# A batched float32 matmul on one Trainium2 core: the last row tile of the first x sent as transfers of four, five and six partitions and one of 48

## The chip, the cores and the metric

The kernel runs on one core of a Trainium2 chip. The metric is the device time of one execution in microseconds (us), lower is better; a time is the median of several executions, and their range is given. "Span" is the profiled execution from its first to its last instruction; it is about 1.8 us shorter than the time that is measured from outside. All multi-run results here were classed as the fast state by the run records. A profile shows one execution only, and a single run is of unknown state.

Ratios are computed as the mean time of one kernel's runs over the mean time of the other's runs of the same rounds.

## The reference

```python
def setup_inputs():
    batch, m, k, n = 32, 512, 1024, 768
    return {"x": np.random.randn(batch, m, k).astype(np.float32),
            "weight": np.random.randn(batch, k, n).astype(np.float32)}

def reference(x, weight):
    return np.matmul(x, weight).astype(np.float32)
```

There are 32 independent products of a 512x1024 with a 1024x768 matrix. Everything has to come from memory once and go back once: the profile counts 167.77 MB read and 50.33 MB written.

## The kernel before

Loads of x and of the weights go out on the GpSimd queue, which converts float32 to bfloat16 on the way, and stores of all but the last four batches go out there too. One load is different. The first x is brought in as float32 on SyncE's queue, in three parts: its first three row tiles (128 partitions x 3 rows), then 96 rows of the last row tile in sixteen transfers of six, then its last 32 rows in one. A "row" in this text is one partition's share of that last row tile: 1024 float32, 4096 bytes.

```python
    def load_x(b):
        xs[b] = x_pool.tile([P, MT, K], BF16, name="x_sb")
        nc.gpsimd.dma_start(out=xs[b], in_=x_view[b])
    # ... load_w(b): the weights of batch b, the same way
    # ... transpose, matmuls, evacuate: TensorE transposes, bf16 matmuls, copies out of PSUM

    with tc.manual_schedule():
        x_first = first_pool.tile([P, MT, K], F32)

        nc.sync.dma_start(x_first[:, :MT - 1], x_view[0, :, :MT - 1])
        for block in range(0, 96, 24):
            for at in range(block, block + 4):
                few = slice(at, block + 24, 4)          # six partitions, four apart
                nc.sync.dma_start(x_first[few, MT - 1], x_view[0, few, MT - 1])
        nc.sync.dma_start(x_first[96:, MT - 1], x_view[0, 96:, MT - 1])
        load_w(0)
        # ... identity; loads of x 1, w 1, x 2, w 2, x 3
        for b in range(B):
            # ... loads ahead and stores behind, on the GpSimd queue
            if b == B - 1:          # six stores of the last four batches go on SyncE's queue
                nc.sync.dma_start(out_view[b - 1, :, halves[0]], outs[b - 1][:, halves[0]])
                for late in range(B - LATE, B - 2):
                    nc.sync.dma_start(out_view[late], outs[late])
                nc.sync.dma_start(out_view[b - 1, :, halves[1]], outs[b - 1][:, halves[1]])
            # ... transposes and matmuls of batch b; after each pair of the last batch:
            #     nc.sync.dma_start(out_view[b, :, halves[pair]], outs[b][:, halves[pair]])
```

SyncE's queue thus carries 1 + 17 + 6 = 24 transfers. The framework gives them eight completion semaphores in turn, so the ninth transfer waits for the first one's semaphore, and so on. The first transposes wait for all sixteen strided transfers, although they read other row tiles.

Of the kernel before, what the change touches and what calls it, by code (L numbers as in the profile page):

```python
# [12 lines left out]
@with_exitstack  # L13
def kernel(
    ctx: ExitStack,
    tc: tile.TileContext,
    x: bass.AP,
    weight: bass.AP,
    out: bass.AP,
):  # L20
    nc = tc.nc
    B, M, K = x.shape
    _, _, N = weight.shape
    P = 128
    MT = M // P
    KT = K // P
    JT = KT // 2
    N2 = 2 * N
    CHUNKED = {B - 4: (4, 4), B - 3: (4, 4), B - 2: (4, 4), B - 1: (4, 2, 2)}
    AHEAD = 3  # L30
    LATE = 4
    HELD = 3

    const = ctx.enter_context(tc.tile_pool(name="const", bufs=1))
    first_pool = ctx.enter_context(tc.tile_pool(name="first", bufs=1))
    w_pool = ctx.enter_context(tc.tile_pool(name="w", bufs=4))
    x_pool = ctx.enter_context(tc.tile_pool(name="x", bufs=5))
    xT_pool = ctx.enter_context(tc.tile_pool(name="xT", bufs=8))
    out_pool = ctx.enter_context(tc.tile_pool(name="out", bufs=7))
    tpsum = ctx.enter_context(tc.tile_pool(name="tpsum", bufs=2, space=bass.MemoryType.PSUM))  # L40
    mpsum = ctx.enter_context(tc.tile_pool(name="mpsum", bufs=2, space=bass.MemoryType.PSUM))



    w_view = weight.rearrange("b (ki ko) n -> b ki ko n", ki=P)
    x_view = x.rearrange("b (mi mo) k -> b mi mo k", mi=P)
    out_view = out.rearrange("b (mi mo) n -> b mi (mo n)", mi=P)

    xs, ws, outs = {}, {}, {}

    def banks():
        return [mpsum.tile([P, 512], F32, name=f"pm{i}") for i in range(3)]
# [5 lines that stand above are left out]
    def load_w(b):  # L58
        ws[b] = w_pool.tile([P, KT, N], BF16, name="w_sb")
        at = 0  # L60
        for n in CHUNKED.get(b, (KT,)):
            nc.gpsimd.dma_start(out=ws[b][:, at:at + n, :], in_=w_view[b, :, at:at + n, :])  # L62
            at += n

    def transpose(b, mt):

        pt = tpsum.tile([P, JT, P], F32, name="pt")
        pairs = xs[b].bitcast(F32)
        for j in range(JT):
            nc.tensor.transpose(pt[:, j, :], pairs[:, mt, j::JT], ident)  # L70
        xT = xT_pool.tile([P, JT, P, 2], BF16, name="xT")
        nc.vector.tensor_copy(  # L72
            xT.rearrange("p j m r -> p (j m r)"), pt.bitcast(BF16).rearrange("p j m -> p (j m)")
        )
        return xT

    def transpose_first(mt):

        xT = xT_pool.tile([P, JT, P, 2], BF16, name="xT")
        for h in range(2):  # L80
            pt = tpsum.tile([P, JT, P], F32, name="pt")
            for i in range(JT):
                nc.tensor.transpose(pt[:, i, :], x_first[:, mt, JT * h + i::KT], ident)  # L83
            nc.vector.tensor_copy(  # L84
                xT[:, 2 * h:2 * h + 2].rearrange("p j m r -> p j r m"),
                pt.rearrange("p (j r) m -> p j r m", r=2),
            )
        return xT



    SPLITS = (
        ((0, 0, 0, 512), (1, 0, 512, N - 512)),
        ((1, N - 512, 0, 1024 - N), (2, 0, 1024 - N, N2 - 1024)),
    )

    def matmuls(pm, half, xT, b, kos, together):
        for ko in kos:
            for i, (bank, at, off, size) in enumerate(SPLITS[half]):
                shares = half == 1 and i == 0  # L100
                nc.tensor.matmul(  # L101
                    pm[bank][:, at:at + size],
                    xT[:, ko // 2, :, ko % 2],
                    ws[b][:, ko, off:off + size],
                    start=(ko == 0 and not (together and shares)),
                    stop=(ko == KT - 1),
                    skip_group_check=together,
                )

    def evacuate(b, pair, pm):  # L110
        o = outs[b][:, pair * N2:(pair + 1) * N2]
        nc.scalar.copy(o[:, 0:512], pm[0])  # L112
        nc.vector.tensor_copy(o[:, 512:1024], pm[1])  # L113
        nc.scalar.copy(o[:, 1024:N2], pm[2])  # L114

    with tc.manual_schedule():
        x_first = first_pool.tile([P, MT, K], F32)

        nc.sync.dma_start(x_first[:, :MT - 1], x_view[0, :, :MT - 1])
        for block in range(0, 96, 24):  # L120
            for at in range(block, block + 4):
                few = slice(at, block + 24, 4)
                nc.sync.dma_start(x_first[few, MT - 1], x_view[0, few, MT - 1])
        nc.sync.dma_start(x_first[96:, MT - 1], x_view[0, 96:, MT - 1])
        load_w(0)
        ident = const.tile([P, P], F32)
        make_identity(nc, ident)
        for b in range(1, AHEAD):
            load_x(b)
            load_w(b)  # L130
        load_x(AHEAD)

        pending = []
        for b in range(B):
            if b + AHEAD + 1 < B:
                load_x(b + AHEAD + 1)
            if b + AHEAD < B:
                load_w(b + AHEAD)
            if b <= B - LATE:
                if b > 0:  # L140
                    pending.append(b - 1)
                if b + AHEAD < B - HELD or b == B - LATE:
                    for at in pending:
                        nc.gpsimd.dma_start(out=out_view[at], in_=outs[at])  # L144
                    pending = []
            if b == B - 1:
                halves = [slice(pair * N2, (pair + 1) * N2) for pair in range(2)]
# [4 lines that stand above are left out]
            outs[b] = out_pool.tile([P, MT * N], F32, name="out_sb")  # L152
            if b not in CHUNKED:
                turn = transpose if b else lambda _, mt: transpose_first(mt)
                xT = {mt: turn(b, mt) for mt in (0, 1)}
                for pair in range(2):
                    pm = banks()
                    for half in range(2):
                        if pair == 0:
                            matmuls(pm, half, xT[half], b, range(KT), False)  # L160
                            xT[2 + half] = turn(b, 2 + half)
                        else:
                            matmuls(pm, half, xT[2 + half], b, range(KT), False)
                    evacuate(b, pair, pm)
                continue
            xT = {0: transpose(b, 0)}
            pms = [banks() for _ in range(2)]
            at = 0
            for n in CHUNKED[b]:
                last = at + n == KT  # L170
                for mt in range(MT):
                    if mt + 1 not in xT and mt + 1 < MT:
                        xT[mt + 1] = transpose(b, mt + 1)
                    matmuls(pms[mt // 2], mt % 2, xT[mt], b, range(at, at + n), True)
                    if last and mt % 2 == 1:
                        pair = mt // 2
                        evacuate(b, pair, pms[pair])
                        if b == B - 1:
                            nc.sync.dma_start(out_view[b, :, halves[pair]], outs[b][:, halves[pair]])
                at += n  # L180
# [30 lines left out]
```

## Time and profile before

| | before |
|---|---|
| median of 6 runs (range) | 517.36 us (516.30 to 517.49) |
| span of the profiled run | 515.7 us |
| memory traffic | 423 GB/s over the span |
| DMA engines, share of busy time | 90% or more in 38 of 40 slices |
| first transpose | 33.6 us |
| first and last increment of the last store | 508.21 and 514.34 us |

The page of the kernel before, parts 1 to 3. The digits are 40 equal slices of the span in tenths of busy time; part 3 has packets, MB and share of 16 engines for each queue.

```profile
span 515.7 us, 5952 instructions
...
PE   0039999999999988779879779887898976999990
...
DMA  8999999999999999999999999999999999999996
...
q0 software_dynamic: 13824, 126.88, 96.7%
q1 hardware_dynamic: 1248, 8.39, 4.1%
q8 instruction: 20, 0.33, 0.2%
...
HBM read 167.77 MB, written 50.33 MB: 423 GB/s over the span
```

The DMA line is what bounds the kernel: nine tenths and more from the second slice to the last but one. TensorE (PE) starts only in the third slice and has gaps. Note the small line of q8: 20 packets of instructions, 0.2% of the engines' time.

The view of waits of the kernel before (engine, line, what it waited for: us in total, times, longest):

```profile
PE pm L101 <- DMA w_sb<-in_weight_dram: 43.9, 17, 4.4
...
PE pt L83 <- DMA x_first<-in_x_dram: 33.6, 1, 33.6
```

TensorE waits for weights that are late, and at the start for the small pieces of the first x.

SyncE's timeline of the kernel before (start us, us, what):

```profile
0.74 0.39 SPq L119 DMA_DIRECT2D x_first<-in_x_dram  x1
1.19 20.33 SPq L123 DMA_DIRECT2D x_first<-in_x_dram  x16
22.62 0.36 SPq L124 DMA_DIRECT2D x_first<-in_x_dram  x1
```

The share of busy time does not say which of the 16 engines ends last. The semaphore increments do, since each transfer gets one increment from every engine that it uses. The trace records them with their times, but not with the engine's number. Below are increments of three transfers on the GpSimd queue and of the last store, as the first increment's time and the others' delay behind it, sorted:

```
before
load at  14.10  0.08 0.22 0.33 0.40 0.42 0.43 0.50 0.50 0.54 0.77 0.83 0.85 0.87 0.89 0.99
load at  43.59  0.06 0.23 0.31 0.37 0.39 0.41 0.47 0.48 0.51 2.74 2.78 2.82 2.84 2.86 2.97
load at  55.73  0.07 0.24 0.32 0.37 0.45 0.46 0.47 0.48 0.51 2.74 2.80 2.81 2.85 2.95 3.93
last st 508.21  0.29 0.53 2.71 2.79 2.81 2.92 2.94 3.15 3.19 3.39 3.54 3.71 3.97 4.81 6.13
```

At 43.59 us six engines are about 2.5 us behind the other ten: those that carried the small transfers. By 55.73 us one of the six is a further 1.1 us late (2.86 to 3.93); one 16 KB instruction packet had passed at 49.7 us. In this trace none of it is made up: at 123.80 us four of the late engines still stand at 2.73 to 2.85 us, and the first increments come in the same rhythm to the end (3.65 to 3.68 us for each store, for example). Each load and store of the GpSimd queue increments once from each of the 16 engines, so a delay stays to the end. In the last store one engine is 6.13 us behind. Its tail can be seen in the profile too, in the view by windows (window, length, busy us of the compute engines, TensorE clock, DMA share, GB/s):

```profile
508.00:510.00 2.00, 0.00 (x0) 0.00 (x0) 0.00 (x0) 0.00 (x0) 0.00 (x0) 0.50 0.84 350
510.00:512.00 2.00, 0.00 (x0) 0.00 (x0) 0.00 (x0) 0.00 (x0) 0.00 (x0) 0.50 0.45 187
512.00:514.00 2.00, 0.00 (x0) 0.00 (x0) 0.00 (x0) 0.00 (x0) 0.00 (x0) 0.50 0.07 31
```

From 508 us on nothing computes. From 512 to 514 us a share of 0.07 of 16 engines is about one engine.

### The profile page before, as it was taken

Reading aid. Unit: us, or ns where it says so; the run is one execution under the profiler, and the core shown is the slowest. Engines: PE = TensorE matmul, PEld = TensorE weight load, DVE = VectorE, ACT = ScalarE, POOL = GpSimd, SP = SyncE. Lnnn points to the kernel's source line nnn. Section 1 sums busy time; section 2 is a strip of 40 time slices with the busy share of each in tenths; the row PEclk is TensorE's granted clock in tenths of the full one; section 3 lists DMA queues with packets and bytes.
Section 4 is the critical chain, followed back from the end, with each engine's and each line's share of the span. In section 5 each row is a group of like instructions: output and inputs, shape, how many; then the busy total and the mean of one; then the engine's idle time right before and its main releaser. Section 6 shows DMA issues by size and latency. Waiting matters only on the chain.

```text
span 515.7 us, 5952 instructions
## 1 busy us (share of the span) xinstructions
PE 417.8 (81%) x2528; PEld 276.1 (54%) x2576; DVE 129.9 (25%) x196; ACT 76.2 (15%) x129; POOL 51.7 (10%) x102
## 2 busy tenths in 40 slices
PE   0039999999999988779879779887898976999990
PEld 0036666666666655446546455554564644566660
DVE  0023333333333313122223231322331322133330
ACT  0001111111111111111101111110110111111110
POOL 3000111111001010100101001100111010111000
PEclk9999999999999989899979998898997998899996
DMA  8999999999999999999999999999999999999996
GB/s 234 223 225 216 218 272 275 260 243 270 277 274 268 243 261 278 275 273 248 250 275 276 275 259 244 271 274 276 272 240 260 277 275 272 250 244 214 300 426 257
DMA packets 15097, 135.64 MB, mean 263 GB/s; under 512 B 1760, under 2 KB 1760, under 8 KB 3552
## 3 DMA queue, kind: packets, MB, share of 16 engines
q0 software_dynamic: 13824, 126.88, 96.7%
q1 hardware_dynamic: 1248, 8.39, 4.1%
q8 instruction: 20, 0.33, 0.2%
q14 instruction: 5, 0.04, 0.0%
HBM read 167.77 MB, written 50.33 MB: 423 GB/s over the span
## 4 chain that ended last, share of the span: by engine, by line
DMA 63%; PE 30%; DVE 3%; issue 1%; ACT 0%; POOLq 0%
PE pm L101 27%; DMA w_sb<-in_weight_dram 25%; DMA out_dram<-out_sb 16%; DMA x_sb<-in_x_dram 16%; DMA x_first<-in_x_dram 6%; PE pt L70 2%; DVE out_sb L113 1%; DVE xT L72 1%; PE pt L83 1%; ACT out_sb L114 0%; POOLq L144 0%; POOLq L62 0%; POOLq L56 0%
## 5 line engine op out<-in xcount | busy, mean ns | idle before, releaser
L101 PE MATMUL pm<-w_sb,xT 128*128 128x256 bf16 (+1 forms) x2000 | 363.4, 336 | 51.3 <-DMA w_sb<-in_weight_dram 43.9
L101 PEld LDWEIGHTS <-xT 128*128 128x128 bf16 x2048 | 204.5, 101 | 185.8 <-issue 52.9
L72 DVE COPY xT<-pt 128x1024 bf16<-128x1024 bf16 x124 | 82.9, 689 | 204.3 <-PE pt L70 204.3
L112 ACT COPY out_sb<-pm 128x512 f32<-128x512 f32 x64 | 37.5, 585 | 289.0 <-PE pm L101 289.0
L113 DVE COPY out_sb<-pm 128x512 f32<-128x512 f32 x64 | 44.0, 687 | 128.1 <-PE pm L101 128.1
L70 PEld LDWEIGHTS pt<-ident,x_sb 128*128 128x128 f32 x496 | 72.3, 206 | 6.0 <-issue 0.8
L70 PE MATMUL pt<-ident,x_sb 128*128 128x128 f32 x496 | 74.6, 284 | 0.0
L114 ACT COPY out_sb<-pm 128x512 f32<-128x512 f32 x64 | 37.5, 586 | 137.3 <-PE pm L101 137.2
L62 POOL DMA_DIRECT2D w_sb<-in_weight_dram x37 | 19.8, 534 | 155.7 <-PE pm L101 66.2
L56 POOL DMA_DIRECT2D x_sb<-in_x_dram x31 | 16.5, 532 | 172.9 <-DMA w_sb<-in_weight_dram 115.8
L83 PE MATMUL pt<-ident,x_first 128*128 128x128 f32 x32 | 6.0, 349 | 33.6 <-DMA x_first<-in_x_dram 33.6
L144 POOL DMA_DIRECT2D out_dram<-out_sb x28 | 15.0, 536 | 94.4 <-DMA x_sb<-in_x_dram 57.0
L83 PEld LDWEIGHTS pt<-ident,x_first 128*128 128x128 f32 x32 | 5.0, 202 | 34.2 <-issue 33.5
L84 DVE CAST xT<-pt 128x512 bf16<-128x512 f32 x8 | 5.6, 727 | 40.9 <-PE pt L83 40.7
L112 ACT ACT_TABLE_LOAD x1 | 1.3, 1283 | 0.7 <-PEq L195 0.7
masks.py:199 POOL TENSOR_SCALAR_AFFINE_SELECT ident<-ident 128x128 f32<-128x128 f32 x1 | 0.3, 287 | 0.1
masks.py:197 POOL MEMSET ident<- 128x128 f32 x1 | 0.2, 223 | 0.0
L195 POOL MEMSET const-float32-0.0<- 128x1 f32 x1 | 0.1, 98 | 0.2 <-issue 0.2
L195 POOL MEMSET const-bfloat16-1.0<- 128x1 bf16 x1 | 0.1, 101 | 0.0
L195 POOL MEMSET const-uint8-127<- 128x1 uint8 x1 | 0.1, 101 | 0.0
L195 POOL MEMSET const-float32-1.0<- 128x1 f32 x1 | 0.1, 98 | 0.0
## 6 DMA issues: line engine op xcount, KB each, us to landing
w_sb<-in_weight_dram POOLq DMA_DIRECT2D x28, 1536.0 KB, 43.2
out_dram<-out_sb POOLq DMA_DIRECT2D x28, 1536.0 KB, 41.9
x_sb<-in_x_dram POOLq DMA_DIRECT2D x31, 1024.0 KB, 39.6
w_sb<-in_weight_dram POOLq DMA_DIRECT2D x7, 768.0 KB, 31.4
out_dram<-out_sb SPq DMA_DIRECT2D x4, 768.0 KB
out_dram<-out_sb SPq DMA_DIRECT2D x2, 1536.0 KB
x_first<-in_x_dram SPq DMA_DIRECT2D x1, 1536.0 KB
w_sb<-in_weight_dram POOLq DMA_DIRECT2D x2, 384.0 KB, 28.1
```

What stands on the lines that cost most here:

```text
L56: nc.gpsimd.dma_start(out=xs[b], in_=x_view[b])
L62: nc.gpsimd.dma_start(out=ws[b][:, at:at + n, :], in_=w_view[b, :, at:at + n, :])
L70: nc.tensor.transpose(pt[:, j, :], pairs[:, mt, j::JT], ident)
L72: nc.vector.tensor_copy(xT.rearrange("p j m r -> p (j m r)"), pt.bitcast(BF16).rearrange("p j m -> p (j m)"))
L83: nc.tensor.transpose(pt[:, i, :], x_first[:, mt, JT * h + i::KT], ident)
L84: nc.vector.tensor_copy(xT[:, 2 * h:2 * h + 2].rearrange("p j m r -> p j r m"), pt.rearrange("p (j r) m -> p j r m", r=2),)
L101: nc.tensor.matmul(pm[bank][:, at:at + size], xT[:, ko // 2, :, ko % 2], ws[b][:, ko, off:off + size], start=(ko == 0 and not (together an ...
L112: nc.scalar.copy(o[:, 0:512], pm[0])
L113: nc.vector.tensor_copy(o[:, 512:1024], pm[1])
L114: nc.scalar.copy(o[:, 1024:N2], pm[2])
L144: nc.gpsimd.dma_start(out=out_view[at], in_=outs[at])
L195: nc = _bacc.Bacc("TRN2", target_bir_lowering=False, num_devices=1)
```

## The change

The intent is to even out the engines: the same 128 rows, fewer of them on the engines that end late.

```diff
-        for block in range(0, 96, 24):
-            for at in range(block, block + 4):
-                few = slice(at, block + 24, 4)
-                nc.sync.dma_start(x_first[few, MT - 1], x_view[0, few, MT - 1])
-        nc.sync.dma_start(x_first[96:, MT - 1], x_view[0, 96:, MT - 1])
+        at = 0
+        for few, times in ((4, 2), (5, 1), (6, 1)):
+            for _ in range(times):
+                for first in range(at, at + 4):
+                    rows = slice(first, at + 4 * few, 4)
+                    nc.sync.dma_start(x_first[rows, MT - 1], x_view[0, rows, MT - 1])
+                at += 4 * few
+        for rows in (slice(at, 80), slice(80, P)):
+            nc.sync.dma_start(x_first[rows, MT - 1], x_view[0, rows, MT - 1])
```

Take it that a transfer of k rows, for k up to 16, runs on the k lowest engines, as the prediction does. Then the rows of the last row tile fall on the engines like this (and the queue has 25 transfers in place of 24):

| engines | 0 to 3 | 4 | 5 | 6 to 15 |
|---|---|---|---|---|
| before | 18 | 18 | 18 | 2 |
| changed | 20 | 11 | 7 | 3 |

## The prediction

> **What bounds it now.** The DMA engines, throughout. The page's slices show them about 90% busy or more; memory traffic is 423 GB/s over the 515.7 us span. TensorE is 81% busy and waits 43.9 us in total for weights (view of waits). The semaphore increments of the GpSimd queue's transfers show more: each transfer gets 16, one per engine. The earliest one keeps a fixed rhythm to the end (about 4.85 us for an x load, 7.28 for weights, 3.66 for a store), so the foremost engine is never starved. Others fall behind and never catch up:
>
> - At 14.1 us all 16 come within 0.99 us. At 43.6 us ten lie within 0.51 us and six are 2.74 to 2.97 us late: those carrying the sixteen six-partition transfers (six 4096-byte packets each). So 16 extra rows cost about 2.5 us, 0.155 us a row.
> - Later delays follow 16 KB instruction packets (20 on the page), one engine at a time, about 1.1 us each. Packets 1, 9 and 17 hit the same one of the six; a second of the six is hit by 8 KB ones.
> - Last store: increments from 508.21 to 514.34 us. The latest engine trails by 6.13 us, the second by 4.81, the third by 3.97. In the last 1.3 us one engine alone moves data.
>
> The kernel ends when one overloaded engine ends, plus 1.4 us of closing barrier.
>
> **What the change does.** It moves the same bytes. Rows of the last tile per engine now: engines 0-5 18, 6-15 2. After: 0-3 20, 4 11, 5 7, 6-15 3. This takes it that a transfer of k rows runs on the lowest k engines (Trainium skill, "DMA: Bandwidth & Descriptors", "Why a DMA increments its semaphore by 16 and not by 1"); the trace agrees in count (six packets, six late increments) and does not number engines. My inference: the latest engine is number 5 and the second 4. It fits that eight engines are hit in turn, that only one of them is among the six, and that it comes first (5 to 12).
>
> **Costs.**
> - Engine 5: 11 rows fewer, 11 x 0.155 = 1.7 us; lateness 6.13 to about 4.4.
> - Engine 4: 7 fewer; 4.81 to about 3.7.
> - Engines 0-3: 2 more, +0.3 us; about 3.5. Engines 6-15: one more, +0.16; at worst 4.1.
> The last engine is still 5, so all 1.7 us is on the critical path.
> - SyncE issues 18 transfers for 17, 0.66 us each, reusing eight semaphores as before. The first transpose waits for the sixteen strided transfers (33.48 us); engines 0-3 still take all 16, so it starts at 33 to 34.5 us. The 48-row transfer lands at about 36 to 39 us, ahead of the last row tile's transposes (44.5 us). No cost.
> - Compute: unchanged. The last matmul (502.6 us) follows the weights, up to 1.7 us earlier.
>
> **Predicted: 515.6 us** (517.28 - 1.7), range 514.6 to 516.9. Faster by over 2%: 0.005; within 2%: 0.985; slower: 0.01.
>
> **What would show it.** Right: the last store's increments spread over about 4.4 us, not 6.1; after startup four engines, not six, are late by about 2.7 us; first transposes within 1 us of 33.5; the span shrinks by about 1.7 us, all in the last stores. Wrong: a spread near 6 (if the latest is engine 4, the gain is about 1 us; if one of 0-3, a loss of 0.3 us), or a first transpose after 36 us.
>
> **What would make it wrong.** Instruction packets falling on other engines in the new program; runs differ by 1.1 us already, most of the gain.

## The result

| | before | changed |
|---|---|---|
| median | 517.36 us, 6 runs | 516.92 us, 6 runs |
| all runs | 517.46 517.28 516.35 517.49 517.44 516.30 | 517.03 516.91 516.92 516.92 516.94 516.88 |
| span of the profile | 515.7 | 515.2 |
| first transpose | 33.57 us | 33.64 us |
| last store, first and last increment | 508.21, 514.34 | 508.40, 513.45 |
| from the last increment to the end of the span | 1.4 us | 1.8 us |

The ratio is 0.9998, with a 95% interval of 0.9985 to 1.0011: the same. The medians differ by 0.44 us, a quarter of the forecast. The runs of before fall into two groups about 1.1 us apart, four near 517.4 and two near 516.3; those of the changed kernel all lie within 0.15 us, between the two groups.

The page of the changed kernel, the same parts:

```profile
span 515.2 us, 6001 instructions
...
PE   0039999999999988798978879977898978989980
...
DMA  8999999999999999999999999999999999999996
...
q0 software_dynamic: 13824, 126.88, 96.7%
q1 hardware_dynamic: 1232, 8.39, 4.1%
q8 instruction: 20, 0.33, 0.2%
...
HBM read 167.77 MB, written 50.33 MB: 423 GB/s over the span
```

Nothing of size has moved; the page is too coarse for this change. (The 16 packets fewer on q1 are four-byte semaphore writes: fewer engines take part.) SyncE's timeline of the changed kernel, with two more transfers in its last line than the one of before:

```profile
0.74 0.38 SPq L119 DMA_DIRECT2D x_first<-in_x_dram  x1
1.18 20.43 SPq L125 DMA_DIRECT2D x_first<-in_x_dram  x16
22.69 2.31 SPq L128 DMA_DIRECT2D x_first<-in_x_dram  x2
```

The end in windows, changed kernel:

```profile
508.00:510.00 2.00, 0.00 (x0) 0.00 (x0) 0.00 (x0) 0.00 (x0) 0.00 (x0) 0.50 0.85 356
510.00:512.00 2.00, 0.00 (x0) 0.00 (x0) 0.00 (x0) 0.00 (x0) 0.00 (x0) 0.50 0.50 209
512.00:514.00 2.00, 0.00 (x0) 0.00 (x0) 0.00 (x0) 0.00 (x0) 0.00 (x0) 0.50 0.03 12
```

The tail of 512 to 514 us has shrunk from 0.07 to 0.03: it is there, but shorter. The increments say who makes it:

```
changed
load at  43.77  0.06 0.24 0.31 0.33 0.36 0.37 0.39 0.41 0.46 0.73 1.34 3.01 3.05 3.08 3.19
load at  55.92  0.05 0.27 0.32 0.33 0.35 0.41 0.42 0.43 0.49 1.33 1.81 3.00 3.04 3.08 3.18
load at 115.47  0.29 0.35 0.40 0.43 0.45 0.52 1.31 1.44 1.55 1.70 1.81 2.99 3.06 3.09 3.19
load at 123.98  0.26 0.31 0.36 0.37 0.40 0.46 1.33 1.42 1.53 1.72 1.83 3.03 3.05 3.08 3.85
last st 508.40  0.28 0.73 2.33 2.61 2.68 2.87 2.87 3.03 3.38 3.42 3.50 3.79 3.88 3.99 5.05
```

At 43.77 us the engines stand in the order of the table above: four near 3.1 (20 rows), one at 1.34 (11 rows), one at 0.73 (7 rows). That is within 0.3 us of where the forecast's 0.155 us a row puts them (an estimate: 2.9, 1.5 and 0.9, counted from the ten engines with three rows, which stand at 0.29 us on average). The engine at 0.73 takes the first 16 KB packet and stands at 1.81 afterwards, so the engine that ended last before is number 5, as inferred, and it ends at about 4.0. But the 8 KB packet at 119.7 us moves one of the four heavy ones (3.19 to 3.85), and those at 294 and 476 us move the latest engine again (to 4.51 and 5.05). That engine is last at the end, at 5.05. It was second before, at 4.81, and the prediction had taken it for engine 4.

There is a second difference. SyncE closes the program with waits on its semaphores, always in the same order. In the view of SyncE's waits, before first and the changed kernel second:

```profile
SPq L206 <- DMA out_dram<-out_sb: 10.3, 5, 2.4
```

```profile
SPq L210 <- DMA out_dram<-out_sb: 11.2, 2, 7.8
```

Before, it waits five times, for one store after another as they end. In the changed kernel it waits only twice, and one wait takes 7.8 us: it stands at the last store's semaphore and has all the others still to ask when that one is complete. One transfer more has dealt the last store the first semaphore in the order.

### The profile page after: what moved, and what is told of

It reads as the page before. It is cut to its first block, busy times and chain, and to the rows that moved or that the text cites. A ratio compares the mean times of both kernels' runs of the same rounds, so it can differ in the third digit from the quotient of the medians.

```text
span 515.2 us, 6001 instructions
## 1 busy us (share of the span) xinstructions
PE 419.6 (81%) x2576; PEld 275.7 (54%) x2576; DVE 129.8 (25%) x196; ACT 76.2 (15%) x129; POOL 51.7 (10%) x102
## 4 chain that ended last, share of the span: by engine, by line
DMA 69%; PE 25%; DVE 2%; issue 1%; ACT 0%; POOLq 0%
DMA w_sb<-in_weight_dram 31%; PE pm L101 22%; DMA out_dram<-out_sb 16%; DMA x_sb<-in_x_dram 15%; DMA x_first<-in_x_dram 6%; PE pt L70 2%; PE pt L83 1%; DVE out_sb L113 1%; DVE xT L72 1%; ACT out_sb L112 0%; ACT out_sb L114 0%; POOLq L62 0%; POOLq L148 0%; POOLq L56 0%
```

## The experiments

Two theories follow. **Theory 1:** the time is the total load of the engine that ends last; the changed kernel ends with an engine of 0 to 3 that the 8 KB packets hit; 0.43 us are lost again in the closing waits; and before's second group of runs is one 16 KB packet fewer on engine 5. **Rivals:** the closing order costs nothing and the 1.1 us is noise; or the end is set by TensorE or by the issue of the last stores, so that rows do not matter.

All twelve runs, four of them repeats of the kernel before, were correct. Every run with several executions is classed the same as before, within 2%, so what the experiments decide they decide by traces and by differences of under 0.3%. Ratios that are not given below: control 0.9999 (0.9987 to 1.0012), rot_before 1.0006 (0.9994 to 1.0019), uniform 1.0005 (0.9993 to 1.0017), uniform_late 1.0019 (1.0006 to 1.0031), stair 0.9992 (0.9976 to 1.0008), bal16 1.0015 (1.0003 to 1.0026).

The rows per engine are worked out as above. A transfer whose rows don't divide by 16 uses fewer engines: the one of 70 rows (stair) posted 14 increments, those of 52 (after_52) and 65 (relieve3) 13 each.

| run | 0 | 1 | 2 | 3 | 4 | 5 | 6 to 12 | 13 | 14, 15 | transfers |
|---|---|---|---|---|---|---|---|---|---|---|
| before, control, rot_before | 18 | 18 | 18 | 18 | 18 | 18 | 2 | 2 | 2 | 24, 24, 25 |
| changed | 20 | 20 | 20 | 20 | 11 | 7 | 3 | 3 | 3 | 25 |
| after_52 | 20 | 20 | 20 | 20 | 12 | 8 | 4 | 0 | 0 | 24 |
| uniform, uniform_late | 8 | 8 | 8 | 8 | 8 | 8 | 8 | 8 | 8 | 8 |
| stair | 21 | 21 | 17 | 13 | 9 | 7 | 5 | 5 | 0 | 24 |
| bal16 | 12 | 12 | 12 | 12 | 12 | 8 | 6 | 6 | 6 | 16 |
| relieve3 | 21 | 21 | 21 | 11 | 11 | 8 | 5 | 0 | 0 | 24 |
| relieve3b | 20 | 20 | 20 | 10 | 10 | 8 | 4 | 4 | 4 | 24 |

### control, control2, control3, control4: the kernel before again

No edit.

> The kernel before, unchanged. Its six times so far were 517.28 to 517.49 (four) and 516.30, 516.35 (two). Theory 1 (one 16 KB instruction packet more or less on the engine that ends last): two separate speeds about 1.1 us apart, near 517.4 and 516.3, nothing between; in a profile of the slow kind the last store's increments spread over 6.1 us, in one of the fast kind over about 5. Rival (noise of the chip): times spread evenly between 516.3 and 517.5.

> The kernel before once more, to catch a profile of its fast kind (516.35; one in three). If fast, theory 1: engine 5 is hit by two 16 KB packets, not three, and the last store's increments spread over about 5 us. Rival: the spread is 6.1 as in the slow kind and the time goes elsewhere. If slow: as the profile of before.

> The kernel before again, for a profile of its fast kind (about 516.35 us). If fast, theory 1: the 16 KB packets come in another turn (the order of their durations, 893 893 949 945 935 975 974 961 ns, is a cycle of eight that starts elsewhere), two of them meet engine 5, the last store's increments spread over about 5 us. Rival: a spread of 6.1 as in the slow kind. If slow: as before.

> The same as the run before it, for the same purpose: a fast profile (516.35 us) should have two 16 KB packets on engine 5 and a last spread near 5 us; a slow one (517.4) three and 6.1 us.

Measured: the control's five runs were 517.45, 516.63, 516.43, 517.46, 517.43; the 11 runs of before beside it included 516.34, 516.41 and 516.42, 516.76 between the groups, and one at 517.86. Two groups are clear, though not perfectly empty between. The three single looks (state unknown) gave 517.50, 517.45 and 517.47 us (spreads of the last store 6.11, 6.04 and 5.96 us). So every profile that I have of this kernel, five of them, is of the slow kind, and the fast kind was never caught. What its last engine does stays an inference.

One of the five profiles bears on it all the same. In the control the cycle of 16 KB packets, told by the order of their durations, starts elsewhere: its first packet moves one of the ten light engines (to 1.58 at 55.76 us), and the latest engine is moved by the third, eleventh and nineteenth (to 3.90, 4.75 and 5.88). That is again three packets, and the same time, 517.45 us. So the start of the cycle does vary between executions of the same kernel, but no profile of this kernel shows two packets on the latest engine.

### rot_before: one transfer more, no row moved

```diff
-        nc.sync.dma_start(x_first[96:, MT - 1], x_view[0, 96:, MT - 1])
+        for rows in (slice(96, 112), slice(112, P)):
+            nc.sync.dma_start(x_first[rows, MT - 1], x_view[0, rows, MT - 1])
```

> The kernel before with its last 32 rows sent as two transfers of 16, so every engine carries the same rows as before, but there is one transfer more and the eight completion semaphores are dealt out one place further. Theory 1 (the last store's semaphore is now the one that the closing sequence waits for first, so seven more waits of 0.06 us follow the last landing): the last landing stays at 514.3 us, the barrier after it grows from 1.4 to 1.8 us, and each speed is 0.43 us slower: 517.85 and 516.75. Rival (the order of the closing waits is free): 517.4 and 516.3.

Measured: 517.62 us median of six runs: 517.90, 517.92, 517.98 and 516.80, with 517.34 and 517.20 between; before in the same rounds 517.41. The last increment of the last store came at 514.32 us, as in the control, and the span grew from 515.7 to 516.1 us. SyncE's closing waits, as starts in the trace:

```
control      114 at 512.492  115 at 514.339                                              span 515.7
rot_before   107 at 514.336  109 at 514.397  110 at 514.461 ... 115 at 514.765           span 516.1
```

In the control the last store's semaphore is number 115, the last to be asked; in this run it is 107, and seven more waits of 0.06 us follow. The view of SyncE's waits of this run has the same form as that of the changed kernel:

```profile
SPq L207 <- DMA out_dram<-out_sb: 10.7, 2, 8.2
```

The slow group rose by 0.45 to 0.5 us, and so did the lowest run. The ratio of the means does not resolve it; the trace does: the same last increment and 0.43 us more behind it. The closing order costs what theory 1 says.

### after_52: the changed kernel with one transfer fewer

```diff
-        for rows in (slice(at, 80), slice(80, P)):
-            nc.sync.dma_start(x_first[rows, MT - 1], x_view[0, rows, MT - 1])
+        nc.sync.dma_start(x_first[at:, MT - 1], x_view[0, at:, MT - 1])
```

> The changed kernel with its last 4 and 48 rows in one transfer of 52, so the count of transfers is that of before; engines 0 to 3 carry 20 rows as in the changed kernel, 4 and 5 one more, 13 to 15 none. Theory 1: last landing as in the changed kernel, about 513.4 us, a closing barrier of 1.4 us in place of 1.8, time 516.5. Rival (the order of the closing waits is free): 516.9.

Measured: 516.47 us, all five runs within 516.43 to 516.51; before in the same rounds 516.34 to 517.86, ratio 0.9988 (0.9976 to 0.9999). The last increment came at 513.36 us against 513.45, so the engines end as in the changed kernel, and the closing waits are five again:

```profile
SPq L209 <- DMA out_dram<-out_sb: 10.8, 5, 3.5
```

So the changed kernel gives 0.45 us away in its closing waits (the comparison with its 516.92 us is across calls, and rows have moved a little too; the traces have 0.44 us less after the last increment). The narrow range is a second finding. In these very rounds before shows two groups and this kernel one, and it differs from before above all in engines 4 and 5. That fits the reading that engine 5's packets make the groups.

### uniform: eight rows on every engine

```diff
-        for block in range(0, 96, 24):
-            ... (the sixteen small transfers)
-        nc.sync.dma_start(x_first[96:, MT - 1], x_view[0, 96:, MT - 1])
+        nc.sync.dma_start(x_first[:, MT - 1], x_view[0, :, MT - 1])
```

> The whole last row tile in one transfer over all 16 engines: 8 rows each, no small transfers. Theory 1 (the time is the total of the engine that is loaded most, 0.155 us a row): the engine that was latest in before has 10 rows fewer (6.13 to about 4.6 us behind), the worst of 6 to 15 has 6 more (3.97 to about 4.9), the two of 0 to 3 that were late fall back to about 3.3 or less; last landing about 513.1 us, time about 516.1; first transposes start right after the first 1.5 MB, near 10 us. Rival (the end is set by TensorE or by the issue of the last stores, so rows do not matter): 517.4.

Measured: 517.32 us (517.24 to 517.57). A miss of 1.2 us. The first transposes started at 10.27 us, as expected. In the last store seven engines, the foremost among them, lay within 0.65 us, but the last four were 4.01, 4.11, 4.21 and 4.80 us behind, and the last increment came at 514.11 us, not 513.1. In this profile the 16 KB packets began elsewhere in their cycle. I had moved rows in my estimate from the profile of before, whose worst engine of 6 to 12 was 3.97 us behind; here those that the packets hit are later than that. The increments fit the packets: twenty of them in a cycle of eight come three times to four engines (4.01 to 4.80) and twice to four others (2.25 to 2.89). Even rows leave the uneven packets.

### uniform_late: the same with TensorE's start put off

```diff
-        ident = const.tile([P, P], F32)
-        make_identity(nc, ident)
+        made = const.tile([P, P], F32)
+        make_identity(nc, made)
+        ident = const.tile([P, P], F32)
 ...
         load_x(AHEAD)
+        nc.vector.tensor_copy(ident, xs[2].bitcast(F32)[:, 0, 0:P])
+        nc.vector.tensor_copy(ident, made)
```

> The uniform run with TensorE's start put off: the identity is copied, by VectorE, only after the load of the third x has landed (about 34 us), with 8 rows on every engine as before. It asks why uniform came out 1.2 us over its expectation of 516.1. Theory A (TensorE starting at about 10 to 15 us instead of 33.5 sets the pace of the early issues badly and costs the 1 us): about 516.2, last landing near 513.1. Theory B (the start does not matter; the 16 KB packets and smaller delays on engines 6 to 12, which carry 6 rows more than in before, end it): 517.3 as in uniform.

Measured: 517.68 us (517.24 to 518.87), first transposes at 33.59 us, last increment 514.32 us. Theory A is out: the early start is not what made uniform slow. Theory B is not shown by that: the runs spread over 1.6 us, and the median is 0.4 us over its value.

### stair: which engine is it?

```diff
+        at = 0
+        for few, n in ((2, 4), (3, 4), (4, 4), (5, 2), (6, 2)):
+            for first in range(at, at + n):
+                rows = slice(first, at + n * few, n)
+                nc.sync.dma_start(x_first[rows, MT - 1], x_view[0, rows, MT - 1])
+            at += n * few
+        for n in (70,):
+            nc.sync.dma_start(x_first[at:at + n, MT - 1], x_view[0, at:at + n, MT - 1])
+            at += n
```

(in place of the seventeen transfers of before)

> A staircase to tell the engines apart: the last row tile goes out as sixteen strided transfers of 2, 2, 2, 2, 3, 3, 3, 3, 4, 4, 4, 4, 5, 5, 6, 6 partitions and one of 70, so that engines 0 and 1 carry 21 rows, 2 17, 3 13, 4 9, 5 7, 6 to 13 5, 14 and 15 none (24 transfers in all, as in before). Both theories: at about 44 us the six late engines stand on a staircase, about 3.2, 3.2, 2.6, 2.0, 1.4 and 1.1 us behind the foremost. Theory 1 (the second-latest engine of before, the one that the 8 KB instruction packets hit near 120, 294 and 478 us, is one of 0 to 3): these packets move one of the upper four steps, and the kernel ends with it: last landing near 513.5 us if it is 0 or 1, at most 513 if it is 2 or 3. Rival (it is engine 4, as predicted): they move the step at 1.4 us, which ends near 3.5.

```
stair
load at  43.69  0.09 0.41 0.46 0.67 0.72 0.73 0.76 0.79 0.81 0.85 1.08 1.93 2.60 3.09 3.16
load at 115.41  0.12 0.38 0.66 0.73 0.73 0.80 1.06 1.70 1.74 1.78 1.87 2.05 2.65 3.06 3.15
load at 123.89  0.08 0.41 0.68 0.76 0.81 0.83 1.08 1.74 1.78 1.84 1.91 2.67 2.73 3.11 3.17
last st 510.09  0.03 0.26 1.00 1.17 1.23 1.58 1.66 1.81 1.83 1.98 2.20 2.49 2.86 2.89 3.37
```

The staircase stands at 43.69 us: 3.16 and 3.09 (engines 0 and 1), 2.60 (2), 1.93 (3), 1.08 (4); the step of engine 5 is not apart from the engines with five rows. The two engines without a row are foremost. This shows, for transfers of two to six partitions, that a transfer of k partitions uses a nested set of k engines. Between 115 and 124 us, where the 8 KB packet passes at 119 us, one engine goes from about 1.9 or 2.0 to about 2.7, while the steps of 4 (1.08), 2 (2.65) and 0 and 1 (3.06, 3.15) stay. Engine 5 also stands near 1.9 by then, having taken its first 16 KB packet; but in the changed kernel the engine that is hit is one of the four with 20 rows. Both together leave number 3, and relieve3 below confirms it. The prediction's engine 4 is out.

Measured: 516.40 us median of four runs, 516.02 to 517.39; last increment at 513.46 us, near the value for 0 or 1 and over the bound of 513 given for 3. The end was not as expected for a reason that I had not foreseen: the foremost engines, which run freely in before, lost time here (first increment of the last store 510.09 us, after 508.21).

### bal16: fewer rows on 0 to 3, even elsewhere

```diff
+        at = 0
+        for few, n in ((5, 4), (6, 2), (16, 2)):
+            for first in range(at, at + n):
+                rows = slice(first, at + n * few, n)
+                nc.sync.dma_start(x_first[rows, MT - 1], x_view[0, rows, MT - 1])
+            at += n * few
+        nc.sync.dma_start(x_first[at:, MT - 1], x_view[0, at:, MT - 1])
```

(in place of the seventeen transfers of before)

> Fewer rows on 0 to 3: four strided transfers of 5 partitions, two of 6, two of 16, one of 64: engines 0 to 4 carry 12 rows, 5 8, 6 to 15 6 (16 transfers in all, so the last store has the semaphore that is waited for last, as in before). Theory 1 (the changed kernel ends with one of 0 to 3 that carries 20 rows, at 0.155 us a row): that engine ends 8 rows or 1.2 us earlier, engines 6 to 12 three rows or 0.5 us later, the last landing is at 512.6 to 513.0 us and the time 515.9 to 516.2. Rival (some other engine or an issue time ends the kernel): 516.5, the time of the changed kernel with 24 transfers, or, if an early start of TensorE costs what it may have cost in the uniform run, about 517.

Measured: 517.80 us (516.82 to 518.03). A miss, like uniform. The last increment came at 514.67 us, and one single engine made it: 5.45 us behind, the next one 3.70. The latest engine gained about 1.1 us with each of the 16 KB packets at 221 and 425 us. These are the ninth and the seventeenth, and the first, at 36.8 us, had moved one of the ten engines with six or eight rows to 1.60 us. By the cycle of eight the engine that ended bal16 is that one, with six rows, and not one of 0 to 3 (read from the cycle, not numbered by the trace). But the delay of the latest engine had also grown from 1.64 us at 44 us to 2.94 us at 116 us, and a packet's 1.1 us would not fill that; what else delayed it is open.

### relieve3 and relieve3b: relieve engine 3

```diff
# relieve3, in place of the seventeen transfers of before, with the loops of stair
+        for few, n in ((3, 10), (5, 3), (6, 3)):     # then one of 65
# relieve3b
+        for few, n in ((3, 10), (5, 2), (6, 4)):     # then one of 64
```

> Relieves engine 3 alone: ten strided transfers of 3 partitions, three of 5, three of 6 and one of 65, so that engines 0 to 2 carry 21 rows, 3 and 4 11, 5 8, 6 to 12 5, 13 to 15 none; 24 transfers, sixteen of them strided, as in the run with the 52-row transfer, where 0 to 3 carry 20, 4 12, 5 8, 6 to 12 4, 13 to 15 none. Theory 1 (that run ended with engine 3, 4.81 us behind the foremost, the next one 4.04): engine 3 ends 9 rows or 1.4 us earlier, near 3.4, another engine ends the kernel at about 4.1 us behind, last landing 512.6 to 512.8 us, time 515.7 to 516.0, and with engine 5 light the times are not in two groups. Rival (the late one is another engine of 0 to 2): it carries one row more, last landing 513.5, time 516.6.

> As the run that relieves engine 3 (515.74 to 516.97 there; its profile, of the 516.97 run, showed the foremost engines, 13 to 15 with no row at all, losing 2 us from 170 us on), with no engine left empty: ten strided transfers of 3 partitions, two of 5, four of 6, one of 64: engines 0 to 2 carry 20 rows, 3 and 4 10, 5 8, 6 to 15 4. Theory 1: engine 3 near 3.3 us behind the foremost at the end, the last one at 3.7 to 4.1, last landing 512.3 to 512.7 us, time 515.6 to 515.9. If the loss of the foremost engines came from their having no rows, all runs are within 0.2 us; if it comes and goes by itself, some runs are again up to 1 us longer. Rival for the changed kernel (another engine of 0 to 2 ended it): 516.5.

Measured: relieve3 516.03 us (515.74, 515.78, 516.03, 516.25, 516.97), ratio to before 0.9982 (0.9968 to 0.9996); relieve3b 516.17 us (515.82 to 516.39), ratio 0.9983 (0.9970 to 0.9997). The rival, which expected 516.5 to 516.6, fails on both medians and on nine of the ten runs. The tenth, 516.97 us, is the one of relieve3 that was profiled: its last increment came at 513.83 us, later than either theory had it (512.6 to 512.8, or 513.5), because its foremost engine came in only at 510.27. So relieve3's profile cannot show the gain, and its five runs spread over 1.2 us where one group had been expected. What the trace does show is who is hit. The 8 KB packet of this run passed at 118.12 us:

```
relieve3
load at 115.37  0.02 0.18 0.39 0.71 0.78 0.80 1.53 1.69 1.79 1.83 1.94 2.09 3.23 3.23 3.30
load at 123.84  0.04 0.17 0.43 0.76 0.82 0.85 1.59 1.86 1.92 2.00 2.12 2.40 3.23 3.24 3.28
```

The three engines with 21 rows, 0 to 2, stay at 3.23 to 3.30, and one of the others rises to 2.40. In the changed kernel the engine that is hit is one of 0 to 3. It is number 3.

Taking rows from engine 3 makes the median shorter than the 516.47 of after_52, by 0.3 to 0.4 us, though the comparison is across calls (the slow group of before stood near 517.4 in each). The profile of relieve3b, window view of the end:

```profile
508.00:510.00 2.00, 0.00 (x0) 0.00 (x0) 0.00 (x0) 0.00 (x0) 0.00 (x0) 0.50 0.99 412
510.00:512.00 2.00, 0.00 (x0) 0.00 (x0) 0.00 (x0) 0.00 (x0) 0.00 (x0) 0.50 0.58 243
512.00:514.00 2.00, 0.00 (x0) 0.00 (x0) 0.00 (x0) 0.00 (x0) 0.00 (x0) 0.50 0.04 15
```

From 508 to 510 us all engines are still at work (0.99, after 0.84 in before): the end is more even. The last store spreads over only 3.01 us:

```
relieve3b
last st 510.14  0.05 0.14 0.86 1.31 1.33 1.34 1.39 1.55 1.67 1.90 2.04 2.25 2.33 2.87 3.01
```

But its last increment is at 513.15 us, not at 512.3 to 512.7, because the foremost engines came in at 510.14 us and not at 508.5. They lost most of the 1.6 us between about 270 and 435 us, where the rhythm of the first increments slipped by up to 0.24 us at a time. At each of these places seven transfers had been issued and not begun, so it was not for want of issued work. The loss is not tied to engines without rows either, since here every engine has at least four. Where it comes from is open. It is why relieve3b gained only 0.30 us on the 516.47 of after_52, where 0.6 to 0.9 had been computed.

## Why the prediction was right or wrong

The forecast was 515.6 us, within 514.6 to 516.9; measured were 516.92 us. The direction was right only against the larger group of runs, which the forecast had taken for the whole, and the size was wrong.

- **Right: what bounds the kernel, and what a row costs.** The end is the end of the last DMA engine. The four heavy engines of the changed kernel, the one at 1.34 and the one at 0.73 stood at 43.77 us within 0.3 us of where the rows put them, and the engine that the first packet hits, the last one of before, carried 7 rows, so it was number 5. Its delay at the end fell from 6.13 to 3.99 us (forecast 4.4).
- **Right: no cost at the start.** First transposes at 33.64 us after 33.57; the 48-row transfer's last increment came at 38.46 us, well before it is used.
- **Wrong step: "the latest engine is number 5 and the second 4".** The second is number 3. It got two rows more, not seven fewer. "Engines 0-3 ... about 3.5" was the mis-sized term: the last of them measured 5.05 us. If the second had been engine 4, engine 5 would have ended the kernel at 508.40 + 3.99 = 512.39 us; engine 3 ended it at 513.45 us. That is 1.06 us of the 1.95 us that engine 5 gave. The increments of stair and relieve3 show which engine it is, and the medians of both relieve3 runs are shorter.
- **Missing step: the closing waits.** "SyncE issues 18 transfers for 17 ... No cost" was wrong by 0.45 us. The eight semaphores are dealt in turn, and one transfer more gave the last store the semaphore that the closing sequence asks first. Shown both ways: one transfer more in before lengthened the span by 0.45 us with the last increment in place; one fewer in the changed kernel won 0.45 us.
- **Not worked in: the two kinds of runs of before.** The forecast named the 1.1 us between runs among the things that could make it wrong, but took 517.28 and one trace for the whole. One run in three of before is 1.1 us faster. Against that kind the changed kernel is 0.6 us slower, and that is why the ratio is 0.9998 while the medians differ by 0.44 us. With fewer rows on engine 5 the two groups are gone in the changed kernel (within 0.15 us) and in after_52 (within 0.08 us). That engine 5 takes one 16 KB packet fewer in the fast kind fits the size of the gap, but no profile shows it.

The sum for the slow kind, from the two profiles: 1.95 us from engine 5, less 1.06 us for engine 3, less 0.43 us of waits (seven of 0.06), is 0.46 us; the spans differ by 0.5 us.

Still open: the fast kind of before was not profiled, and neither the additional delay of single engines in uniform and bal16 nor the loss of the foremost engines in stair and the relieve3 runs has an explanation.

## What to carry to other kernels

When the DMA engines are busy from end to end, look at each engine's own finish, by the spread of the semaphore increments of the last transfers, not at the mean share: a few 4 KB rows and instruction packets decide which engine is last, and moving load only pays down to the next engine. Find out which engine that is with a staircase of loads before relying on an order of engines. And count the transfers of a queue whose semaphores are dealt in turn: the one that ends last should also be the one that the closing sequence asks last.

## What the Trainium skill lacked or had wrong

- "Runtime: NRT & Kernel Launch", "Instruction fetch mechanics", calls the cost of crossing a 16 KiB instruction block "mostly hidden". Here, if the 20 packets that the profile calls "instruction", of 16,384 bytes each, are such blocks, each delayed one DMA engine by about 1.1 us (2.86 to 3.93 us behind after the one at 49.7 us in before), several fell on the same engine, and in a DMA-bound kernel that is 3 us at the end. The page does not say which DMA engines carry the blocks; here they come to eight in turn.
- "DMA: Bandwidth & Descriptors", "Why a DMA increments its semaphore by 16 and not by 1", has SyncE's transfers on the lowest-numbered k engines. The stair run agrees with nested sets of engines for k of 2 to 6 (steps of 3.1, 2.6, 1.9 and 1.1 us behind at 43.69 us); the numbers themselves no trace shows.
- The same page, "Latency and other measured facts", names engines 7 and 15 as the usual slow ones. In before, the ten engines with two rows, 7 and 15 among them by that numbering, lay within 0.51 us at 43.59 us, and the late engines were 5 and 3, for their rows and packets.
- No page has the cost of the closing waits: 0.06 us for each semaphore still to be asked after the last landing, 0.43 us for seven.
- No page tells a strided from a contiguous partition range in the issue time on SyncE: in the changed kernel's trace four partitions four apart took 0.58 us, four next to each other 0.29 us, 48 next to each other 0.33 us.
